# A hybrid decoder step: decode attention in visits of two page tiles, with page loads issued from GpSimd into five buffers

## The chip, the cores and the metric

The kernel runs on one core of a Trainium2 chip. Time is device time of the whole program in microseconds. Engine names: PE is TensorE (matmuls), PEld its weight loads, DVE is VectorE, ACT is ScalarE, POOL is GpSimd, SP is SyncE, whose queue issues most DMAs.

## The reference

One layer of a decoder trunk for a prompt of 512 tokens and 8 samples that each decode one token behind a past of 2048. Cut to the part that the change touches, attention of the samples over their paged caches:

```python
PAST_LEN, PAGE_SIZE, DEC_BATCH, A_HEADS, A_HD = 2048, 128, 8, 4, 64   # 16 pages a sample
...
# k_all, v_all: the cached rows of a sample's pages (by page_table), then the new token's
p1 = jax.nn.softmax(jnp.einsum('bqhd,bkhd->bhqk', qb1, k1f) + bias, axis=-1)
p2 = jax.nn.softmax(jnp.einsum('bqhd,bkhd->bhqk', qb2, k2f) + bias, axis=-1)
return jnp.einsum('bhqk,bkhe->bqhe', p1 - lam * p2, vf)
```

Around it stand a combined projection `z = h @ w_in` (58 column tiles of 128), attention over the prompt, two convolutions, a gated MLP, four gates, a merge, cross attention and a feed-forward network. All inputs are float32.

## The kernel before

Tokens lie along the free dimension, 520 of them (512 and 8), in two halves of 260. A column tile of a weight matrix is 128 columns wide; `gemm` multiplies it in three passes (high by high, high by low, low by high part), 48 matmuls of 260 columns for a full tile, all recorded at L219. Three weight tiles are loaded ahead (`LA`), and ScalarE (L179) and VectorE (L180) split each into its two parts. These tiles form one stream, `order`, and set the pace of TensorE.

Everything else is hung on that stream in stages. `run` emits a column tile, then `take` hands what follows on its sums to a list, and each later tile moves the older ones a stage on. Decode attention is a generator, `decode` (L475 on), and `step(n)` moves it on by n visits. `ZS[n]` says how many visits follow column tile n of the first 26; `G1`, `G3`, `G2` say it for the tiles of three branch gates, where one visit also follows each gate tile.

A visit of the scores part (L500) multiplies one page tile, that is four pages of 128 keys for one sample, by the queries of four heads: four float32 products with 32 rows of output each, into one bank `d`. Each product shows in the trace as two records. After eight samples VectorE takes the bank up (L503). A visit of the values part (L549) multiplies the tile of four pages by the probabilities `Dt`, again four products. There are 32 page tiles of keys and 32 of values, 128 products each. The context `behind()` keeps a product after the newest column tile, but does not keep the four of a visit together; the scheduler of the framework may place products of the prompt's attention (scores L597, transposes L632, values L646, norm L653) or of a norm's column sums (L242) between them. L730 are the transposes of V.

A page tile is loaded by four DMAs of 256 KB (`fetch`, L463 to L466): an entry of the page table `pt` is read into a register, then the DMA is issued, both on the SP queue, in which the loads of the weight tiles (L176) also stand. Page tiles share three buffers (tag `pg`) with the score tile `Sd`, so two hold pages during the scores and three during the values; a load waits for the products that read the buffer before. On GpSimd's queue stand a few fills and four loads of x for a later stage (L1154).

Of the kernel before, what the change touches and what calls it, by code (L numbers as in the profile page):

```python
# [31 lines left out]
ZS = [0, 0, 0, 1, 1, 0, 3, 1, 3, 2, 1, 2, 1, 2, 3, 1, 2, 1, 2, 1, 0, 1, 1, 1, 0, 1]  # L32
WARM = 2
SQ = 4
G2 = [0, 0, 1, 2, 0, 0, 0, 1]
G1 = [1, 0, 1, 0, 0, 0, 1, 0]
G3 = [1, 0, 0, 0, 0, 0, 1, 0]
# [17 lines left out]
# columns of the packed constants  # L55
# [40 lines left out]
def layer(ctx: ExitStack, tc: tile.TileContext, I: dict, O: dict):  # L96
# [12 lines left out]
    # ---------------------------------------------------------------- helpers  # L109
# [73 lines left out]
    def first_weights():  # L183
        """the first tile of the stream, in parts that come between those of x"""
# [18 lines left out]
    def pin():  # L203
        """what VectorE has been given since the last sums were taken up stays behind that."""
# [23 lines left out]
    def gemm(ps, W, xs, first=True, last=True, k0=0, apart=False):  # L228
        """both halves of the tokens; apart: one after the other"""
# [6 lines left out]
    def colsum(mat, srcs):  # L236
        """mat^T (sum of srcs over partitions) in float32: two halves with their columns."""
# [8 lines left out]
    def rsqrt(src, n, v, y, a):  # L246
        """v = (src / n + EPS) ** -0.5, with one Newton step: v (3 - x v^2) / 2."""
# [19 lines left out]
    def rstd(mat, srcs, n, y, v=None):  # L267
        """the reciprocal deviations from column sums; y is scratch."""
# [4 lines left out]
    # ---------------------------------------------------------------- constants  # L273
# [6 lines left out]
    lamt = cst.tile([P, 256], F32, name="lamt")  # L280
# [10 lines left out]
    # ---------------------------------------------------------------- x: split, norm  # L291
# [5 lines left out]
    for i in range(WARM):          # the array's clock rises while the first loads come in  # L297
# [41 lines left out]
    lp = cst.tile([P, 128], F32, name="lamp")  # L339
# [3 lines left out]
    def parameters():  # L343
        """the little columns made from the parameters"""
# [32 lines left out]
    def advance():  # L377
        """the newest sums are taken up, then what is left of the older ones goes a stage on."""
# [10 lines left out]
    def go():  # L389
        """a stage of everything"""  # L390
# [6 lines left out]
    def flush():  # L397
        """everything that is left"""
# [3 lines left out]
    def take(post):  # L402
        """what follows on a tile's sums is begun behind the next tile."""
# [5 lines left out]
    def run(name, i, src, post, steps=0, k0=0, W=None, apart=False):  # L409
        """one column tile"""  # L410
# [7 lines left out]
    def pair(names, src, posts):  # L418
        """the first two column tiles, together while the rows of src come in"""
# [21 lines left out]
    def headnorm(z, sq, mat, n, g):  # L441
        """z * g * rsqrt(mean over the rows of mat's blocks)"""
# [16 lines left out]
    # ---------------------------------------------------------------- paged decode attention  # L459
    last = []  # L460

    def fetch(dst, src, i):
        """dst = the page that entry i of the page table names."""  # L463
        with tc.issue_after(last[-1].ins) if last else nullcontext():
            pid = SP.value_load(pt[0:1, i:i + 1], min_val=0, max_val=159)
        last.append(SP.dma_start(out=dst, in_=src[bass.ds(pid, 1)].rearrange("o p f -> p o f")))  # L466

    def pages():
        return dp.tile([P, 4, 512], F32, tag="pg", name="pg", bufs=3)
# [3 lines left out]
    def decode():  # L473
        Sd = dp.tile([P, 2048], F32, tag="pg", name="Sd", bufs=3)
# [14 lines left out]
        held = [loadk(0)]  # L489
        yield  # L490
        held.append(loadk(1))
        yield
        for n in range(32):
            g, s = n // NS, n % NS
            if s == 0:
                ps = dtile()
            kp = held.pop(0)
            with behind():
                for h in range(4):
                    PE.matmul(ps[32 * h:32 * h + 32, :], lhsT=qz[:, s * 128 + 32 * h:s * 128 + 32 * h + 32],  # L500
                              rhs=kp[:, :, h * P:h * P + P], start=s == 0, stop=s == NS - 1)
            if s == NS - 1:
                V.tensor_tensor_reduce(out=Sd[:, 512 * g:512 * g + 512], in0=ps, in1=cv("dbias"), scale=1.0,  # L503
                                       scalar=-3e38, op0=ALU.add, op1=ALU.max, accum_out=sd[:, g:g + 1])
            held.append(loadk(n + 2) if n < 30 else loadv(n - 30))
            yield
        # the new token's own score
# [32 lines left out]
        held.append(loadv(2))  # L540
        yield
        os_ = []
        for n in range(32):
            if n % 16 == 0:
                ps = dtile()
            vp = held.pop(0)
            with behind():
                for i in range(4):
                    PE.matmul(ps[32 * i:32 * i + 32, :], lhsT=Dt[:, n % 16, :], rhs=vp[:, i, :], start=n % 16 == 0,  # L549
                              stop=n % 16 == 15)  # L550
            if n % 16 == 15:
# [3 lines left out]
            if n + 3 < 32:  # L555
                held.append(loadv(n + 3))
# [44 lines left out]
    def difference(h, qt, ps):  # L601
        """of the two softmaxes"""
# [20 lines left out]
    def turned(h, qt, d):  # L623
        """the keys of one tile of queries on the partitions"""
# [13 lines left out]
    def values(h, pr, dh, dl):  # L638
        """times v, and the norm of the head"""
# [23 lines left out]
    def attention():  # L663
        """a stage a tile: the scores of some queries, the turning of those before, their values, their norm"""
# [71 lines left out]
    # ---------------------------------------------------------------- branch B  # L736
# [43 lines left out]
    def center(ys, ps):  # L780
        """subtracts the mean over the 256 channels of two tiles; returns the squares."""
# [9 lines left out]
    # ---------------------------------------------------------------- branch C  # L791
# [164 lines left out]
    # ---------------------------------------------------------------- gates and merge  # L956
# [35 lines left out]
    def gates(i, br, steps):  # L992
        Wb = None
        for c in range(KT):
            pg_, py = gated(i, c)
            ztile(ZG + 8 * i + c, pg_, 1)
# [470 lines left out]
```

## Time and profile before

| what | value |
|---|---|
| median of three runs | 1075.08 us (1074.6 to 1077.41) |
| span of the profiled execution | 1072.4 us |
| TensorE busy | 1062.6 us (99%) |
| VectorE busy | 594.8 us (55%) |
| ScalarE busy | 457.7 us (43%) |
| GpSimd busy | 4.4 us |

The profiled execution's span counts from its first instruction to its last; the runs' times include what lies around that. A matmul's busy time overlaps that of the next, so the price of a group is read from the start of its first record to the start of what follows.

### The profile page before, as it was taken

How to read it: one execution, taken by the hardware profiler on the slowest of the kernel's cores; microseconds unless marked ns; L12 is line 12 of the kernel's file. 1: busy time of each engine (PE TensorE's matmuls, PEld its weight loads, DVE VectorE, ACT ScalarE, POOL GpSimd, SP SyncE). 2: the span in 40 equal slices, each digit the busy share in tenths (PEclk: the TensorE clock that was granted, in tenths of full speed). 3: DMA queues.
4: the chain of work that ended last, by engine and by line, in shares of the span. 5: the costliest groups of instructions: out<-in, count | busy, mean ns of one | idle time of the engine just before them, and what ended most of it. 6: DMA issues, size and time to landing. Idle time of an engine off the chain costs nothing.

```text
span 1072.4 us, 21375 instructions
## 1 busy us (share of the span) xinstructions
PE 1062.6 (99%) x8434; PEld 962.0 (90%) x8434; DVE 594.8 (55%) x1022; ACT 457.7 (43%) x761; POOL 4.4 (0%) x11
## 2 busy tenths in 40 slices
PE   8999999999999999999999999999999999999998
PEld 7967777878988888888999986999999999999998
DVE  6764665775646665534677678754224424445443
ACT  7754565863412225312555586553223213312320
POOL 0000000000000000000010000000000000000000
PEclk9999999999999999999999999999999999999999
DMA  8667777756567777766432556122232232222231
GB/s 280 239 193 215 218 209 221 237 172 181 178 206 237 236 218 235 218 206 216 148 132 86 202 188 239 41 99 91 87 99 90 90 99 86 93 99 82 96 110 50
DMA packets 73861, 172.06 MB, mean 160 GB/s; under 512 B 9633, under 2 KB 12450, under 8 KB 73634
## 3 DMA queue, kind: packets, MB, share of 16 engines
q1 hardware_dynamic: 73442, 169.65, 50.1%
q8 instruction: 66, 1.08, 0.4%
q0 software_dynamic: 320, 1.07, 0.3%
q14 instruction: 33, 0.27, 0.1%
HBM read 165.07 MB, written 5.61 MB: 159 GB/s over the span
## 4 chain that ended last, share of the span: by engine, by line
PE 96%; ACT 1%; DVE 1%; DMA 0%; SPq 0%; issue 0%; DVEq 0%
PE g L219 80%; PE d L500 4%; PE d L549 3%; PE m L242 2%; PE m L597 1%; PE m L219 1%; PE g L1115 1%; PE m L646 1%; PE m L632 0%; PE m L653 0%; DMA hl<-in_xT 0%; PE m L1261 0%; PE d L1196 0%; ACT t L1266 0%; PE m L730 0%; PE m L534 0%
## 5 line engine op out<-in xcount | busy, mean ns | idle before, releaser
L219 PE MATMUL g<-hl,wh 128*128 128x260 f32 x4332 | 709.2, 285 | 1.2 <-ACT hl L324 0.6
L219 PEld LDWEIGHTS g<-hl,wh 128*128 128x128 f32 x4332 | 595.5, 188 | 51.6 <-issue 18.6
L219 PE MATMUL g<-hl,wl 128*128 128x260 f32 x2166 | 437.0, 283 | 0.0
L219 PEld LDWEIGHTS g<-hl,wl 128*128 128x128 f32 x2166 | 334.1, 188 | 1.9 <-issue 1.7
L179 ACT CAST wh<-w 128x1024 fp32r<-128x1024 f32 x154 | 161.4, 1048 | 395.4 <-PE g L219 309.0
L180 DVE TENSOR_TENSOR wl<-w,wh 128x1024 fp32r<-128x1024 f32 x154 | 188.1, 1222 | 160.9 <-ACT wh L179 151.8
L433 DVE TENSOR_TENSOR t<-g,R 128x520 f32<-128x520 f32 x48 | 33.4, 696 | 76.3 <-PE g L219 76.2
L219 PE MATMUL g<-hb,wh 128*128 128x260 f32 (+1 forms) x436 | 71.1, 282 | 0.0
L219 PEld LDWEIGHTS g<-hb,wh 128*128 128x128 f32 x436 | 60.8, 188 | 0.1
L219 PE MATMUL g<-hb,wl 128*128 128x260 f32 (+1 forms) x218 | 46.6, 283 | 0.0
L500 PE MATMUL d<-pg,qz 128*32 128x512 f32 x256 | 44.9, 604 | 0.4 <-DVE qz L702 0.4
L143 ACT CAST hl<-t 128x520 fp32r<-128x520 f32 (+2 forms) x42 | 24.4, 581 | 43.2 <-DVE t L1331 27.5
L827 DVE SCALAR_TENSOR_TENSOR hl<-uc,cols,hl 128x512 f32<-128x512 f32 x60 | 41.4, 745 | 0.0
L1345 DVE TENSOR_TENSOR hb<-g,hb 128x520 f32<-128x520 f32 x16 | 11.2, 700 | 49.4 <-PE g L219 49.4
L144 DVE TENSOR_TENSOR hl<-t,hl 128x520 fp32r<-128x520 f32 (+2 forms) x42 | 27.0, 644 | 15.8 <-ACT hl L143 15.5
L219 PEld LDWEIGHTS g<-hb,wl 128*128 128x128 f32 x218 | 34.6, 188 | 0.0
L549 PE MATMUL d<-pg,Dt 128*32 128x512 f32 x256 | 33.9, 604 | 0.0
L249 ACT ACTIVATE t<-m,little 128x260 f32<-128x260 f32 (+1 forms) x42 | 19.1, 474 | 26.1 <-PE m L242 13.2
L965 ACT ACTIVATE t<-t 128x520 f32<-128x520 f32 x24 | 15.2, 635 | 27.1 <-DVE t L433 27.0
L254 DVE TENSOR_TENSOR t<-t 128x520 f32<-128x520 f32 (+1 forms) x27 | 15.5, 576 | 19.5 <-ACT t L253 19.1
L1331 DVE TENSOR_TENSOR t<-t 128x520 f32<-128x520 f32 x32 | 22.2, 694 | 0.0
L608 DVE CUSTOM_DVE_ANT_0 t<-m,bias 128x128 f32<-128x128 f32 (+3 forms) x32 | 14.6, 486 | 12.3 <-PE m L597 12.3
(271 smaller groups left out, 818.3 us busy)
## 6 DMA issues: line engine op xcount, KB each, us to landing
pg<-in_kc SPq DMA_DIRECT2D x128, 256.0 KB, 3.4
pg<-in_vc SPq DMA_DIRECT2D x128, 256.0 KB, 3.0
w<-in_win SPq DMA_DIRECT2D x56, 512.0 KB, 4.5
w<-in_wup SPq DMA_DIRECT2D x32, 512.0 KB, 3.3
w<-in_wdn SPq DMA_DIRECT2D x32, 512.0 KB, 3.3
w<-in_wo SPq DMA_DIRECT2D x8, 512.0 KB, 3.3
hl<-in_cmk SPq DMA_DIRECT2D x16, 256.0 KB, 5.2
hl<-in_cmv SPq DMA_DIRECT2D x16, 256.0 KB, 5.5
```

What stands on the lines that cost most here:

```text
L143: S.copy(hi, src)
L144: V.tensor_tensor(out=lo, in0=src, in1=f(hi), op=ALU.subtract)
L179: S.copy(wh, w)
L180: free.add(V.tensor_tensor(out=wl, in0=w, in1=f(wh), op=ALU.subtract).ins.name)
L219: m = PE.matmul(o, lhsT=w, rhs=x[sl], start=first and n == 0, stop=last and n == 2)
L242: PE.matmul(ps[:, 0:H2], lhsT=mat, rhs=s[:, sl], start=i == 0, stop=i == len(srcs) - 1)
L249: S.activation(v[:, sl], i, AF.Identity, scale=-1.0 / n, bias=NEPS)
L433: V.tensor_tensor(out=two(t), in0=gv(ps), in1=two(Rt), op=ALU.mult)
L500: PE.matmul(ps[32 * h:32 * h + 32, :], lhsT=qz[:, s * 128 + 32 * h:s * 128 + 32 * h + 32], rhs=kp[:, :, h * P:h * P + P], start=s == 0, st ...
L549: PE.matmul(ps[32 * i:32 * i + 32, :], lhsT=Dt[:, n % 16, :], rhs=vp[:, i, :], start=n % 16 == 0, stop=n % 16 == 15)
L827: V.scalar_tensor_tensor(out=y[:, 0:NP], in0=u[:, k:k + NP], scalar=cw[:, k:k + 1], in1=y[:, 0:NP], op0=ALU.mult, op1=ALU.add)
L1331: V.tensor_tensor(out=r, in0=r, in1=r, op=ALU.mult)
```

## The change

Visits now take two page tiles: eight products, 16 records, under a raised priority so that the scheduler places nothing between them. There are 16 visits of scores and 16 of values. `fetch` reads the page table and issues the page loads on GpSimd. The tag `pg` has five buffers. `ZS`, `G1`, `G2`, `G3` are new; in the gates visits follow the gate tile alone (`steps[c]`, or every second for the fourth gate). The two parameter tiles `lamt` and `lp` and the tile `Rm` move to shared pools, and the scratch for GpSimd's DMAs is 2048 bytes. Comments are gone, so lines shift by a few: L500 stays, L549 becomes L551, L597 becomes L599, L632 becomes L634, L730 becomes L732.

```diff
-ZS = [0, 0, 0, 1, 1, 0, 3, 1, 3, 2, 1, 2, 1, 2, 3, 1, 2, 1, 2, 1, 0, 1, 1, 1, 0, 1]
+ZS = [0, 0, 0, 1, 0, 1, 1, 1, 1, 1, 1, 1, 1, 1, 1, 1, 0, 1, 1, 1, 0, 1, 1, 0, 1, 0]
...
-            pid = SP.value_load(pt[0:1, i:i + 1], min_val=0, max_val=159)
-        last.append(SP.dma_start(out=dst, in_=src[bass.ds(pid, 1)].rearrange("o p f -> p o f")))
+            pid = GP.value_load(pt[0:1, i:i + 1], min_val=0, max_val=159)
+        last.append(GP.dma_start(out=dst, in_=src[bass.ds(pid, 1)].rearrange("o p f -> p o f")))
...
-        return dp.tile([P, 4, 512], F32, tag="pg", name="pg", bufs=3)
+        return dp.tile([P, 4, 512], F32, tag="pg", name="pg", bufs=5)
...
-            kp = held.pop(0)
-            with behind():
-                for h in range(4):
-                    PE.matmul(ps[32 * h:32 * h + 32, :], lhsT=qz[:, s * 128 + 32 * h:s * 128 + 32 * h + 32],
-                              rhs=kp[:, :, h * P:h * P + P], start=s == 0, stop=s == NS - 1)
+            kps = [held.pop(0) for _ in range(2)]
+            with tc.high_priority(offset=4 * AHEAD), behind():
+                for s, kp in zip((s0, s0 + 1), kps):
+                    for h in range(4):
+                        PE.matmul(ps[32 * h:32 * h + 32, :], lhsT=qz[:, s * 128 + 32 * h:s * 128 + 32 * h + 32],
+                                  rhs=kp[:, :, h * P:h * P + P], start=s == 0, stop=s == NS - 1)
...
-            held.append(loadk(n + 2) if n < 30 else loadv(n - 30))
+            for i in range(2 * v + 4, 2 * v + 6):
+                held.append(loadk(i) if i < 32 else loadv(i - 32))
...
-            ztile(ZG + 8 * i + c, pg_, 1)
+            ztile(ZG + 8 * i + c, pg_, steps[c])
...
-        ztile(ZG + c, post_g0(c), 1)
+        ztile(ZG + c, post_g0(c), c % 2)
...
-    nc = _bacc.Bacc("TRN2", target_bir_lowering=False, num_devices=1)
+    nc = _bacc.Bacc("TRN2", target_bir_lowering=False, num_devices=1, dynamic_dma_scratch_size=2048)
```

The values part changes in the same way as the scores. In the program's order the 128 score products stood in 39 runs (18 of four, 10 of one, 9 of three, one of seven, one of twelve) and now in 16 of eight; the 128 value products in 31 runs (30 of four, one of eight) and now in 16 of eight. The column matmuls stood in 104 uninterrupted runs and now stand in 84. The number of products is 8009 in both.

TensorE, the first visit of decode attention (`qz` are the samples' queries, `pg` a page tile, `d` the bank). Before:

```order
L219 MATMUL g<-hl,wl 128x260 x2
L242 MATMUL m<-t,cc 128x260 x2
L500 MATMUL d<-pg,qz 32x512 x12
L219 MATMUL g<-hl,wh 128x260 x4
L219 MATMUL g<-hl,wl 128x260 x2
```

After:

```order
L219 MATMUL g<-hl,wl 128x260 x2
L500 MATMUL d<-pg,qz 32x512 x8
L242 MATMUL m<-t,cc 128x260 x2
L219 MATMUL g<-hl,wh 128x260 x4
L219 MATMUL g<-hl,wl 128x260 x2
```

The visit moved ahead of the two column sums and has two page tiles in place of three.

TensorE, the score products around the second group of the prompt's scores (`t` holds its probabilities, which L632 turns). Before:

```order
L242 MATMUL m<-t,cc 128x260 x2
L597 MATMUL m<-hl 128x384 x6
L632 MATMUL m<-cc,t 128x128
L500 MATMUL d<-pg,qz 32x512
L632 MATMUL m<-cc,t 128x128 x2
L500 MATMUL d<-pg,qz 32x512 x7
L219 MATMUL g<-hl,wh 128x260 x4
L219 MATMUL g<-hl,wl 128x260 x2
L219 MATMUL g<-hl,wh 128x260 x3
L500 MATMUL d<-pg,qz 32x512 x4
```

After:

```order
L500 MATMUL d<-pg,qz 32x512 x8
L242 MATMUL m<-t,cc 128x260 x2
L599 MATMUL m<-hl 128x384 x6
L634 MATMUL m<-cc,t 128x128
L219 MATMUL g<-hl,wh 128x260 x4
L219 MATMUL g<-hl,wl 128x260 x2
L219 MATMUL g<-hl,wh 128x260 x4
L219 MATMUL g<-hl,wl 128x260
L634 MATMUL m<-cc,t 128x128 x2
```

The single score product between the transposes is gone; matmuls of the column tile stand there.

The queues of the page loads, with the semaphores that each waits for (DMAHW and DMASW count landings of SP's and GpSimd's loads, eight of each in turn; PE and DVE count those engines' work). SP before:

```order
L466 DMA pg<-in_kc 128x512 [waits DMAHW3_49]
L176 DMA w<-in_win 128x1024 [waits DMAHW4_49,DVE_49]
L465 TENSOR_LOAD pt
L465 ISA x2
L466 ISA
L466 DMA pg<-in_kc 128x512 [waits DMAHW5_49]
```

GpSimd after:

```order
L465 DMA pg<-in_kc 128x512 [waits DMASW3_49]
L464 TENSOR_LOAD pt
L464 ISA x2
L465 ISA
L465 DMA pg<-in_kc 128x512 [waits DMASW4_49,PE_49]
```

The table read, its register work and the load moved as they were to GpSimd's queue; weight loads no longer stand between them.

## Rows read from the trace of the kernel before

**Rows 1.** The page: span, busy time by engine, TensorE's granted clock in 40 slices.

```profile
span 1072.4 us, 21375 instructions
...
PE 1062.6 (99%) x8434; PEld 962.0 (90%) x8434; DVE 594.8 (55%) x1022; ACT 457.7 (43%) x761; POOL 4.4 (0%) x11
...
PEclk9999999999999999999999999999999999999999
```

**Rows 2.** The chain that ended last: shares by line; then start us, us, what.

```profile
by line: PE g L219 79.8%; PE d L500 3.9%; PE d L549 3.0%; PE m L242 1.9%; PE m L597 1.2%; PE m L219 1.1%; PE g L1115 0.9%; PE m L646 0.9%; PE m L632 0.5%; PE m L653 0.4%; DMA hl<-in_xT 0.4%; PE m L1261 0.4%; PE d L1196 0.4%; ACT t L1266 0.4
...
33.73 5.74 PE g L219 x48
39.47 1.75 PE m L242 x8
```

**Rows 3.** Timeline, TensorE, one page tile: start us, us, engine line, out<-in, records.

```profile
251.71 0.40 PE L219 MATMUL g<-hl,wl 128*128 128x260 f32 x2
252.04 1.06 PE L500 MATMUL d<-pg,qz 128*32 128x512 f32 x8
253.03 0.75 PE L219 MATMUL g<-hl,wh 128*128 128x260 f32 x4
253.62 0.40 PE L219 MATMUL g<-hl,wl 128*128 128x260 f32 x2
```

**Rows 4.** Timeline, TensorE, value products: two page tiles together.

```profile
487.28 0.40 PE L219 MATMUL g<-hl,wl 128*128 128x260 f32 x2
487.61 1.92 PE L549 MATMUL d<-pg,Dt 128*32 128x512 f32 x16
489.46 0.76 PE L219 MATMUL g<-hl,wh 128*128 128x260 f32 x4
490.06 0.40 PE L219 MATMUL g<-hl,wl 128*128 128x260 f32 x2
```

**Rows 5.** Timeline, TensorE, score products: a page tile split one and three.

```profile
76.05 1.05 PE L500 MATMUL d<-pg,qz 128*32 128x512 f32 x2
77.03 0.44 PE L632 MATMUL m<-cc,t 128*128 128x128 f32 x2
77.39 1.92 PE L500 MATMUL d<-pg,qz 128*32 128x512 f32 x14
79.24 0.74 PE L219 MATMUL g<-hl,wh 128*128 128x260 f32 x4
```

**Rows 6.** Timeline, TensorE, the first run of score products.

```profile
54.40 1.06 PE L500 MATMUL d<-pg,qz 128*32 128x512 f32 x6
55.85 2.76 PE L500 MATMUL d<-pg,qz 128*32 128x512 f32 x18 [0.39 <-DVE qz L702]
58.54 0.74 PE L219 MATMUL g<-hl,wh 128*128 128x260 f32 x4
```

**Rows 7.** Timeline, SyncE's queue: three page loads, nothing else between them.

```profile
240.63 2.56 SPq L466 DMA_DIRECT2D pg<-in_kc  x3
```

**Rows 8.** Line L466, SyncE's page loads: ns min/median/max of the issue.

```profile
L466 SPq DMA_DIRECT2D pg<-in_kc x128: 332/333/955, 23.7 to 264.4; - x128
```

**Rows 9.** Timeline, GpSimd: its four loads in the whole program.

```profile
551.32 2.26 POOL L1154 DMA_DIRECT2D hb<-in_xT  x4
```

**Rows 10.** Line L1154, GpSimd's loads: ns min/median/max, then landing.

```profile
L1154 POOL DMA_DIRECT2D hb<-in_xT x4: 536/536/672, 551.3 to 553.0; - x4
...
DMA to landing us min/median/max: 3.3/3.6/3.9
```

**Rows 11.** Timeline, TensorE: where two groups of V transposes begin.

```profile
64.39 0.27 PE L730 MATMUL m<-cc,t 128*128 128x128 f32 x1
...
140.43 0.27 PE L730 MATMUL m<-cc,t 128*128 128x128 f32 x1
```

**Rows 12.** Groups by line, VectorE, 50 to 145 us: count | busy us, mean ns.

```profile
L433 DVE TENSOR_TENSOR t<-g,R 128x520 f32<-128x520 f32 x8 | 5.5, 692 | 0.0
...
L727 DVE COPY vnew<-t 128x8 f32<-128x8 f32 x3 | 0.5, 162 | 0.0
```

More of the change, by code (lines that the diff above doesn't have):

```diff
@@ L31 @@
 CR = "k0 k1 q0 q1 q2 q3 k2 v0 v1 k3 v2 v3"
-ZS = [0, 0, 0, 1, 1, 0, 3, 1, 3, 2, 1, 2, 1, 2, 3, 1, 2, 1, 2, 1, 0, 1, 1, 1, 0, 1]
+ZS = [0, 0, 0, 1, 0, 1, 1, 1, 1, 1, 1, 1, 1, 1, 1, 1, 0, 1, 1, 1, 0, 1, 1, 0, 1, 0]
 WARM = 2
+G1 = [1, 1, 1, 1, 0, 1, 0, 1]
+G3 = [1, 0, 1, 1, 0, 1, 0, 1]
+G2 = [1, 1, 1, 0, 1, 1, 0, 0]
 SQ = 4
-G2 = [0, 0, 1, 2, 0, 0, 0, 1]
-G1 = [1, 0, 1, 0, 0, 0, 1, 0]
-G3 = [1, 0, 0, 0, 0, 0, 1, 0]
 TB = 10
@@ L279, in layer @@
     stc = cst.tile([P, 2, NS, 30], F32, name="stc")
-    lamt = cst.tile([P, 256], F32, name="lamt")
     pt = cst.tile([1, 128], I32, name="pt")
@@ L338, in layer @@
     lam = cst.tile([P, 8], F32, name="lamc")
-    lp = cst.tile([P, 128], F32, name="lamp")
     LAM, LAMROW = lam[:, 4:5], lam[:, 5:6]
@@ L343, in parameters @@
     def parameters():
+        lamt, lp = T()[:, 0:256], T()[:, 0:128]
         SP.dma_start(out=pt, in_=I["pt"])
@@ L464, in fetch @@
         with tc.issue_after(last[-1].ins) if last else nullcontext():
-            pid = SP.value_load(pt[0:1, i:i + 1], min_val=0, max_val=159)
-        last.append(SP.dma_start(out=dst, in_=src[bass.ds(pid, 1)].rearrange("o p f -> p o f")))
+            pid = GP.value_load(pt[0:1, i:i + 1], min_val=0, max_val=159)
+        last.append(GP.dma_start(out=dst, in_=src[bass.ds(pid, 1)].rearrange("o p f -> p o f")))
     def pages():
-        return dp.tile([P, 4, 512], F32, tag="pg", name="pg", bufs=3)
+        return dp.tile([P, 4, 512], F32, tag="pg", name="pg", bufs=5)
     exps = []
     def decode():
-        Sd = dp.tile([P, 2048], F32, tag="pg", name="Sd", bufs=3)
+        Sd = dp.tile([P, 2048], F32, tag="pg", name="Sd", bufs=5)
         sd = dp.tile([P, 40], F32, tag="sd", name="sd")
@@ L487, in loadv @@
             return vp
-        held = [loadk(0)]
+        held = [loadk(0), loadk(1)]
         yield
-        held.append(loadk(1))
+        held += [loadk(2), loadk(3)]
         yield
-        for n in range(32):
-            g, s = n // NS, n % NS
-            if s == 0:
+        for v in range(16):
+            g, s0 = v // 4, 2 * (v % 4)
+            if s0 == 0:
                 ps = dtile()
-            kp = held.pop(0)
-            with behind():
-                for h in range(4):
-                    PE.matmul(ps[32 * h:32 * h + 32, :], lhsT=qz[:, s * 128 + 32 * h:s * 128 + 32 * h + 32],
-                              rhs=kp[:, :, h * P:h * P + P], start=s == 0, stop=s == NS - 1)
-            if s == NS - 1:
+            kps = [held.pop(0) for _ in range(2)]
[4 more added lines that the diff above has]
+                                  rhs=kp[:, :, h * P:h * P + P], start=s == 0, stop=s == NS - 1)
+            if s0 == NS - 2:
                 V.tensor_tensor_reduce(out=Sd[:, 512 * g:512 * g + 512], in0=ps, in1=cv("dbias"), scale=1.0,
                                        scalar=-3e38, op0=ALU.add, op1=ALU.max, accum_out=sd[:, g:g + 1])
-            held.append(loadk(n + 2) if n < 30 else loadv(n - 30))
+            for i in range(2 * v + 4, 2 * v + 6):
+                held.append(loadk(i) if i < 32 else loadv(i - 32))
             yield
@@ L539, in decode @@
         V.tensor_copy(dn, ps[:, 0:32])
-        held.append(loadv(2))
+        held.append(loadv(4))
         yield
         os_ = []
-        for n in range(32):
-            if n % 16 == 0:
+        for v in range(16):
+            if v % 8 == 0:
                 ps = dtile()
[L546 to L551, printed above, removed]
+            vps = [held.pop(0) for _ in range(2)]
+            with tc.high_priority(offset=4 * AHEAD), behind():
+                for n, vp in zip((2 * v % 16, 2 * v % 16 + 1), vps):
+                    for i in range(4):
+                        PE.matmul(ps[32 * i:32 * i + 32, :], lhsT=Dt[:, n, :], rhs=vp[:, i, :], start=n == 0, stop=n == 15)
+            if v % 8 == 7:
                 ot = T()
@@ L554, in decode @@
                 os_.append(ot)
-            if n + 3 < 32:
-                held.append(loadv(n + 3))
+            for i in range(2 * v + 5, 2 * v + 7):
+                if i < 32:
+                    held.append(loadv(i))
             yield
@@ L1001, in gates @@
                 mpool.append(pool("mp"))
-            Wb = run("wbcd", 2 * (i - 1) + c // 4, br, py, steps[c], k0=2 * (c % 4), W=Wb if c % 4 else None)
+            Wb = run("wbcd", 2 * (i - 1) + c // 4, br, py, 0, k0=2 * (c % 4), W=Wb if c % 4 else None)
     gates(1, bo, G1)
@@ L1043, in layer @@
     ms = []
-    Rm = cst.tile([P, 256], F32, name="Rm")
+    Rm = h2.tile([P, 256], F32, name="Rm")
     Rc = cst.tile([P, 4], F32, name="Rc")
```

## The prediction

> **What bounds the kernel now.** The page comes first [rows 1]: TensorE is busy for 1062.6 of 1072.4 us and its granted clock stands at full speed (2.4 GHz of its two levels) in every slice. The chain of waits agrees [rows 2]: column tiles of the weight stream (L219) hold 79.8% of the span, the score products of decode attention (L500) 3.9%, its value products (L549) 3.0%; DMA has 0.4%, all of it the first load of x. So the program is a queue of TensorE work, and a change is worth what it takes out of that queue, less what it makes TensorE wait for. A column tile of 48 matmuls takes 5.74 us when nothing disturbs it [rows 2], or 0.1196 us each.
>
> **What a visit costs.** Every float32 product of decode attention shows as two records, so a page tile (four products) is 8 records. Look at one alone in a column tile [rows 3]: it starts at 252.04 and the stream goes on at 253.03, 0.99 us later. But the borders cost too. From the last pair ahead (251.71) to the first pair behind (253.62) 1.91 us pass, and the six column matmuls in that stretch need 0.72: the visit's price is 1.19, of which 0.20 are borders. Two page tiles that happen to stand together [rows 4]: 487.61 to 489.46 is 1.85, and 490.06 - 487.28 - 0.72 = 2.06 with borders. So the second page tile costs 0.87, not 1.19. The third price is the surprise of this trace [rows 5]: one single product (2 records) holds TensorE from 76.05 to 77.03, 0.98 us, as long as all four. The seven that follow take 1.85 (77.39 to 79.24), as long as eight, so the three left over cost 0.99. A page tile that is split into one and three pays twice.
>
> **Scores: the sum.** In the order of before the 128 score products stand in 39 runs: 18 of four, 10 of one, 9 of three, one of seven and one of twelve. By the rows this is 18 x 0.99 + 10 x 0.98 + 9 x 0.99 + 1.85 + 4.14 = 42.5 us; the chain's 3.9% of 1072.4 is 41.8, so the count holds. The 4.14 is the first run [rows 6], 54.40 to 58.54: three page tiles in one run are worth 0.99 + 0.86 + 0.86 = 2.71, and 1.43 are a wait, since its fourth product wants the last head's query (qz) and the other three are done too early. In the order of after there are 16 runs of eight: 16 x 1.85 = 29.6. The wait does not go, it grows: the first visit now stands ahead of two L242 products that stood before it. Such a pair takes 0.88 (four of these products, eight records, 1.75 [rows 2]). TensorE gets to the visit that much earlier and qz comes when it came, so I charge 1.43 + 0.88 = 2.3. Scores: 42.5 - 29.6 - 2.3 = 10.6 us saved.
>
> **Values.** 30 runs of four and one of eight before, 30 x 0.99 + 1.85 = 31.6 (the chain: 3.0%, 32.2); 16 x 1.85 = 29.6 after. 2.0 saved.
>
> **Borders.** In the program's order the column stream is cut into 104 runs before and 84 after (same products, 8009 of them in both). Twenty interruptions fewer at 0.20 are 4.0 us. Between zero (if the fewer borders sit beside transposes, where a change of work may cost nothing) and 4.6 (23 score runs fewer) I take 4.0, the price of the plain rows.
>
> **Sum:** 10.6 + 2.0 + 4.0 = 16.6 us.
>
> **What the queues cost.** Taking 256 page loads off SP gives nothing by itself, as no weight load stands in the chain. What matters is whether GpSimd can issue them in time. Each is a table read, some register work and a DMA. On SP three of them cover 2.56 us from the first DMA's start to the last one's end [rows 7], and a DMA takes 0.33 of that [rows 8]: (2.56 - 0.33) / 2 = 1.12 each. All that GpSimd issues in the trace of before is four loads of 260 KB from fixed addresses [rows 9]: 2.26 us for four, 0.536 each at the median, 3.6 us to land [rows 10]. Table reads on GpSimd stand nowhere in this trace, so I bound the price c of one page load there. Below: 0.57, if the reads run ahead while the previous DMA is being written. Above, serial: 1.12 - 0.33 + 0.54 = 1.33. I take the serial end for the test, as the safer.
>
> What c may be follows from the densest stretch. In after the second visit stands right ahead of the first group of V transposes (L730 in before) and the ninth right ahead of the third group; these groups begin at 64.39 and 140.43 in before [rows 11], 76.0 us apart. There before spends 16.7 us on 16 score runs (6 x 0.99, 5 x 0.98, 4 x 0.99, 1.85) and after 7 x 1.85 = 13.0; with about 1 us of borders 71.3 remain for seven visits, 10.2 apart. During the scores four buffers hold pages (the fifth holds the score tile), two visits' worth. The load for visit k may begin when visit k - 2 has read its buffers; GpSimd then needs 8c per visit. From the first visit to the second one L242 pair, one column tile and a visit pass, 0.88 + 5.74 + 2.06 = 8.7 us. Counting from the first visit (k = 0), the pages of the tenth (k = 9) are there after 8 x 8c + 3.6, and it comes after 8.7 + 8 x 10.2 = 90.3. It waits when 64c + 3.6 > 90.3, that is c > 1.35. The tile after it has no visit, and the queue catches up. At 1.33 nothing waits (with 1.6 us to spare), at 1.5 the loss is 9 us, and at c = 1.61 the whole gain of 16.6 is eaten. GpSimd has nothing else to do in this stretch, and behind its last page load stand only a fill and four loads for a later stage. Each load also waits for the eighth one before it to land; 8c is well over 3.6 even at 0.57. The five buffers pay for themselves with room (a smaller DMA scratch, three small tiles moved), which moves no work on TensorE.
>
> **A rule against it.** In the first score stretch VectorE is mostly two-input work of 0.69 us; its plain copies take 0.16 [rows 12]. The Trainium skill, "SBUF — State Buffer", section "Who interferes with whom", says that a GpSimd-issued DMA has its descriptors written through a port that VectorE locks during copies and one-input scalar operations in a fast mode, and that two-input operations leave writes alone. No row here shows it. By that page, as an estimate, a load that met one such copy would wait 0.16 us and be at 1.49, a loss of 9 us inside the first rival below; by the row alone the loss is nothing.
>
> **Rivals.**
> First, supply is tight, or chains come late (chance 0.20). c between 1.35 and 1.6 takes up to 16 us back in the stretch of the first ten visits. Or the transposes of the prompt's attention (L632), which had a split page tile as cover ahead of them, wait for VectorE; the nearest row is the 0.39 us idle at the first visit [rows 6], and at some 16 such places that would be 6 us. For it: VectorE is busy for 55% of the span [rows 1]. Against: ahead of these products the chain gives neither VectorE nor ScalarE a share; the one ScalarE line in it is of cross attention [rows 2]. Either lands between 1062 and 1072; I put it at 1065.
> Second, slower than before (0.10): every GpSimd issue has to wait for one VectorE operation, 0.69 us [rows 12], so c = 1.33 + 0.69 = 2.0. Then the tenth visit is 64 x 2.0 + 3.6 - 90.3 = 41 us late; less 16.6 that is +25, 1100. It decides from c = 1.61 on. Against it speak the four loads of [rows 9, 10], which took 0.54 each.
> Third, the change does not do what it says (0.05): the pair of [rows 4] is a lucky case, and each page tile costs 0.99 wherever it stands. Then 32 x 0.99 = 31.7 replaces each 29.6, the gain falls by 4.2 and the borders' 4.0 go too: 8.4 us are left, 1067. Against: the seven of [rows 5] show the same 0.86 step.
>
> **How the numbers follow.** The profiled span 1072.4 becomes 1055.8. The median of the three runs, 1075.08, lies 2.7 above the span, so 1075.08 - 16.6 = 1058.5. The forecast has 0.63, with its own range of 1055 to 1062 (the borders at 0 on one side, the first wait gone on the other). The full range reaches over most of the first rival and the third: 1054 to 1070; what is left out is the slow case and some 0.08 at the edges. About 0.3% (3.2 us) is what a measurement of this kernel can tell from no change. Faster: 0.63 + 0.05 + most of 0.20, 0.85; same 0.05; slower 0.10.
>
> **What would show it.** In the profile of the changed kernel: L500 and its twin at 2.8% each in the chain; every visit 16 records in 1.85 us; the first one with a wait for qz of about 2.3; no wait of TensorE for a page load; GpSimd's table reads no further apart than 1.35 us when it is not held by a buffer. Wrong would be: TensorE idle ahead of L500 on DMA between 80 and 150 us (supply), or idle at L634 on VectorE or ScalarE (chains).

## The result: 10.9 us saved, 16.6 forecast

The changed kernel takes 1064.3 us (median of four executions, 1061.1 to 1066.7) against 1075.2 for the kernel before: ratio 0.9891, 95% interval 0.9869 to 0.9914. It is 1.1% faster, in the forecast direction and within the range of 1054 to 1070, but 5.8 us above the forecast of 1058.5. Its profiled execution was the longest of the four: span 1065.0, where before's is 1072.4 [rows 1].

**The profile after.** First the page, then the head of the chain that ended last, as in [rows 1, 2]:

```profile
span 1065.0 us, 21390 instructions
...
PE 1049.2 (99%) x8434; PEld 968.2 (91%) x8434; DVE 594.7 (56%) x1022; ACT 455.6 (43%) x759; POOL 142.4 (13%) x267
...
PEclk9999999998899999999999999999999999999999
```

```profile
by line: PE g L219 74.7%; PE d L551 2.8%; PE d L500 2.3%; DMA w<-in_win 1.6%; PE m L242 1.4%; PE m L219 1.1%; PE m L599 1.0%; PE g L1117 0.9%; ACT wh L179 0.7%; issue 0.7%; DVE wl L180 0.6%; ACT t L615 0.5%; ACT t L249 0.4%; PE m L648 0.4%;
```

Two things strike the eye. GpSimd is now busy (its 256 page loads). And TensorE's clock, full in all 40 slices before, is down in the tenth and eleventh, 240 to 293 us; the column stream has lost 5 points of the chain to work that feeds it.

A visit looks as the prediction said. TensorE's timeline, the first visit and the third:

```profile
54.90 3.08 PE L500 MATMUL d<-pg,qz 128*32 128x512 f32 x16
57.91 1.15 PE L242 MATMUL m<-t,cc 128*128 128x260 f32 x4
...
75.00 1.92 PE L500 MATMUL d<-pg,qz 128*32 128x512 f32 x16
76.85 1.14 PE L242 MATMUL m<-t,cc 128*128 128x260 f32 x4
```

76.85 - 75.00 = 1.85, the price of the two page tiles of [rows 4]. All visits but the first score visit and one value visit of 2.01 take it. From each record's start to the next one's, the 256 score records take 30.8 us (42.6 before), the value records 29.8 (31.7 before): 11.75 and 1.9 saved.

So 13.65 us are there in the products alone, and yet the profiled span is only 7.4 shorter. Where the rest went shows when both traces are laid side by side at fixed places of the column stream (start of the product on g that follows the first n, us):

```
n        before    after    after - before
576       114.9    110.3        -4.6
1344      267.0    256.1       -10.9
1536      296.5    294.4        -2.1
3072      522.7    515.3        -7.4   (and the same to the end)
```

Up to the 1344th product all goes as forecast. Between the 1344th and the 1536th, 256 to 294 us in after, 8.8 us are given back. TensorE's timeline there, with its idle time and what ended it:

```profile
256.76 0.64 PE L219 MATMUL g<-hl,wh 128*128 128x260 f32 x4
257.24 0.40 PE L219 MATMUL g<-hl,wl 128*128 128x260 f32 x2
260.17 0.83 PE L219 MATMUL g<-hl,wh 128*128 128x260 f32 x4 [2.53 <-DVE mg L977]
260.79 0.64 PE L219 MATMUL g<-hl,wl 128*128 128x260 f32 x2
261.22 1.07 PE L219 MATMUL g<-hl,wh 128*128 128x260 f32 x4
262.09 0.64 PE L219 MATMUL g<-hl,wl 128*128 128x260 f32 x2
263.52 1.20 PE L219 MATMUL g<-hl,wh 128*128 128x260 f32 x4 [0.80 <-DVE sd L523]
```

TensorE waits for a buffer of sums (g) that VectorE has not taken up: L977 multiplies the branch's sums by the gate. The second wait ends with L523, a step of the softmax's sums; right ahead of it on VectorE stands L432, which takes up a gate's sums (262.69 to 263.38). And after the first wait the same four products take 0.87 us from start to next start (261.22 to 262.09) where they took 0.48 (256.76 to 257.24). ScalarE, at the same time:

```profile
254.42 0.72 ACT L519 ACTIVATE Sd<-Sd,sd 128x512 f32<-128x512 f32 x1 [3.50 <-DVE sd L515]
```

From there the chain that ended last runs through ScalarE and VectorE until TensorE goes on:

```profile
255.24 2.12 ACT Sd L519 x6
...
257.45 1.28 ACT L967
258.75 0.65 ACT t L967
259.41 0.07 DVE mg L977
```

The exponentials of decode attention's softmax (L519, four of 0.7 us) waited until 254.42 for VectorE, where L515 stood among the input work of branch C (L814 to L840); the gate's sigmoid (L967) is ordered behind them in the program, comes with its table load at 257.45 and 258.75, and only then can L977 run. Third, TensorE's busy time and granted clock in stretches of 5 us:

```profile
255.00:260.00 5.00, 2.64 (x23) 1.00 0.24 93
260.00:265.00 5.00, 4.04 (x19) 0.57 0.25 75
265.00:270.00 5.00, 5.00 (x34) 0.75 0.09 33
270.00:275.00 5.00, 5.00 (x44) 0.93 0.12 32
275.00:280.00 5.00, 5.00 (x25) 0.50 0.67 199
```

(Columns: stretch, its length, TensorE busy with records, clock, DMA share, GB/s.) After the idle 2.5 us the clock stands at its lower level (1.2 of 2.4 GHz) from about 261 to 267 us and is full again until 274. Then it is low once more, to 281, and this second time TensorE had been busy since 263.5; what ran there was the row of the sixteen Dt products:

```profile
271.12 3.94 PE L535 MATMUL m<-C,Sd 128*128 128x32 f32 x32
...
275.30 1.21 PE L219 MATMUL g<-hl,wh 128*128 128x260 f32 x4
```

In before every 5 us from 250 to 290 have 5.00 busy and 1.00. Of the 8.8 us, 3.3 are idle time. The visits in this part of the stream weigh about the same in both (after has a pair of value tiles, 1.85; before had one tile of scores and one of values, 1.0 each), so the rest, some 5.5, is the clock. The four executions of after bear this out: mean granted clock 0.994, 0.995, 0.997, 1.000 and spans 1065.0, 1063.4, 1061.8, 1059.4. The one at full clock is 5.6 shorter than the profiled one, and 13.0 below before's profile, 3.6 short of the forecast 16.6: about the idle time.

**Theory:** the visits bring what the sum said; the loss is the softmax, which the new step table puts two gate tiles earlier, among branch C's input work on VectorE and ahead of a gate's sigmoid on ScalarE. **Rivals:** the loss belongs to the visits themselves; or the supply of pages.

### The profile page after: what moved, and what is told of

The parts are those of the page before. It is cut to its first block, busy times and chain, and to the rows that moved or that the text cites. A ratio compares the mean times of both kernels' runs of the same rounds, so it can differ in the third digit from the quotient of the medians.

```text
span 1065.0 us, 21390 instructions
## 1 busy us (share of the span) xinstructions
PE 1049.2 (99%) x8434; PEld 968.2 (91%) x8434; DVE 594.7 (56%) x1022; ACT 455.6 (43%) x759; POOL 142.4 (13%) x267
## 4 chain that ended last, share of the span: by engine, by line
PE 88%; ACT 5%; DVE 3%; DMA 2%; issue 1%; SPq 0%; ACTq 0%; DVEq 0%
PE g L219 75%; PE d L551 3%; PE d L500 2%; DMA w<-in_win 2%; PE m L242 1%; PE m L219 1%; PE m L599 1%; PE g L1117 1%; ACT wh L179 1%; DVE wl L180 1%; ACT t L615 0%; ACT t L249 0%; PE m L648 0%; DMA hl<-in_xT 0%; PE m L1263 0%
## 5 line engine op out<-in xcount | busy, mean ns | idle before, releaser
L219 PE MATMUL g<-hl,wh 128*128 128x260 f32 x4332 | 710.6, 286 | 5.7 <-DVE mg L977 2.5
L219 PEld LDWEIGHTS g<-hl,wh 128*128 128x128 f32 x4332 | 599.7, 189 | 23.6 <-issue 6.4
L219 PE MATMUL g<-hl,wl 128*128 128x260 f32 x2166 | 439.4, 284 | 0.0
L179 ACT CAST wh<-w 128x1024 fp32r<-128x1024 f32 x154 | 161.3, 1048 | 416.1 <-PE g L219 306.8
L219 PEld LDWEIGHTS g<-hl,wl 128*128 128x128 f32 x2166 | 336.2, 190 | 0.2
L180 DVE TENSOR_TENSOR wl<-w,wh 128x1024 fp32r<-128x1024 f32 x154 | 188.1, 1222 | 151.6 <-ACT wh L179 147.8
L465 POOL DMA_DIRECT2D pg<-in_vc x128 | 68.8, 537 | 184.1 <-issue 79.5
L465 POOL DMA_DIRECT2D pg<-in_kc x128 | 69.3, 541 | 146.9 <-issue 101.4
L432 DVE TENSOR_TENSOR t<-g,R 128x520 f32<-128x520 f32 x48 | 33.3, 695 | 68.5 <-PE g L219 68.4
L219 PE MATMUL g<-hb,wh 128*128 128x260 f32 (+1 forms) x436 | 71.1, 282 | 0.0
L219 PEld LDWEIGHTS g<-hb,wh 128*128 128x128 f32 x436 | 60.8, 188 | 0.1
L219 PE MATMUL g<-hb,wl 128*128 128x260 f32 (+1 forms) x218 | 46.6, 283 | 0.0
L219 PEld LDWEIGHTS g<-hb,wl 128*128 128x128 f32 x218 | 34.6, 188 | 0.0
L500 PE MATMUL d<-pg,qz 128*32 128x512 f32 x256 | 31.8, 599 | 0.1
L551 PE MATMUL d<-pg,Dt 128*32 128x512 f32 x256 | 30.8, 598 | 0.0
L249 ACT ACTIVATE t<-m,little 128x260 f32<-128x260 f32 (+1 forms) x42 | 18.9, 474 | 23.8 <-PE m L242 11.5
```

What stands on the lines that cost most here:

```text
L179: S.copy(wh, w)
L180: free.add(V.tensor_tensor(out=wl, in0=w, in1=f(wh), op=ALU.subtract).ins.name)
L249: S.activation(v[:, sl], i, AF.Identity, scale=-1.0 / n, bias=NEPS)
L432: V.tensor_tensor(out=two(t), in0=gv(ps), in1=two(Rt), op=ALU.mult)
L465: last.append(GP.dma_start(out=dst, in_=src[bass.ds(pid, 1)].rearrange("o p f -> p o f")))
L551: PE.matmul(ps[32 * i:32 * i + 32, :], lhsT=Dt[:, n, :], rhs=vp[:, i, :], start=n == 0, stop=n == 15)
```

## The experiments

Times are medians; "before" is the kernel before on the same chip in the same hour, 1075.8 to 1076.7. Ratios are to it.

**1. The softmax two gate tiles later.** In after:

```diff
-G1 = [1, 1, 1, 1, 0, 1, 0, 1]
+G1 = [0, 0, 1, 1, 1, 1, 1, 1]
```

> The kernel after, with the softmax of decode attention (L511 to L520) two gate tiles later, where the kernel before had it; visits, queue and buffers stay. Theory: in the profile of after the softmax's exponentials (L519) wait until 254.4 us for VectorE, hold the gate's sigmoid (L967) and so L977 back, TensorE idles 2.5 and 0.8 us and then runs part of 255 to 282 us at its lower clock; that stretch gave back 8.9 us. Moved, it goes: no wait on L977 of over 0.5 us, granted clock 1.00 from 250 to 300 us, span 1055 to 1058, time 1057 to 1060. Rival: the loss belongs to the visits (the clock falls in this stretch wherever the softmax stands, or the wait only moves with it): span 1062 to 1065, time 1062 to 1066.

1060.7 us, ratio 0.986 (0.984 to 0.988); span 1058.0 in the profile, clock 1.00 from 250 to 300 us. Up to the 1344th product the trace is that of after within 0.6 us; at the 1536th it is 9.0 ahead, at the end 7.0. The span is at the upper end of the theory's range and the time 0.7 above it; its "no wait" failed. TensorE's waits still have

```profile
PE g L219 <- DVE sd L523: 1.7, 1, 1.7
...
PE g L219 <- DVE mg L977: 0.7, 1, 0.7
```

(total us, times, longest). So 2.4 us of idle time are left of 3.3, without a fall of the clock in this execution. Most of the gain over after is the clock: three of the four executions show 1.000, with spans of 1058.0, 1058.5 and 1059.7, and after's one at 1.000 has 1059.4. At equal clock that is about 1 us, the size of the idle time saved. That the later softmax keeps the clock up fits these counts but is not shown by them. The visits are unchanged; whether they bring the rest is left to experiment 5.

**2. Nothing between, but single pages on SyncE's queue.** The kernel before with one thing of the change:

```diff
-            with behind():
+            with tc.high_priority(offset=4 * AHEAD), behind():
                 for h in range(4):
```

(and the same at the value products).

> The kernel before, page loads on SP and visits of one page as they were, with one thing of the change: the products of a page get the priority that keeps other work out. By its order the scores then stand in 29 runs (25 of four, two of eight, one of three and one of nine) instead of 39, and the column stream in 109 runs instead of 104. Theory (a split page tile pays 0.98 us twice): scores 42.5 becomes 25 x 0.99 + 2 x 1.85 + 0.99 + some 3.0 (nine, with its wait) = 32.4, less 10; borders 5 x 0.20 = +1.0; time 1075.2 - 9 = 1066, between 1063 and 1068. Rival (the price is a page tile's, split or not, and only pairs save): time 1074 to 1077.

1068.4 us, ratio 0.993 (0.991 to 0.995). The score records take 32.6 us against 42.6: 10.0 saved, as expected, the time a little above the range, because 3.8 us came in elsewhere, 1.6 of them between the 1344th and the 1536th product, where the clock is down for a moment (0.51 and 0.64 in the stretches from 280 to 284 us). So most of what the change takes out of the score products is the split tile of [rows 5], not the pair. In time the pair is worth about as much: unsplitting gives 8.0 us here (1076.4 to 1068.4), pairs 7.3 in experiments 10 and 11.

**3. After, with its page loads on SyncE's queue.**

```diff
-            pid = GP.value_load(pt[0:1, i:i + 1], min_val=0, max_val=159)
-        last.append(GP.dma_start(out=dst, ...
+            pid = SP.value_load(pt[0:1, i:i + 1], min_val=0, max_val=159)
+        last.append(SP.dma_start(out=dst, ...
```

> The kernel after with its page loads issued from SP again, as in before (five buffers and pair visits stay; by its order two of the 16 score visits fall into two runs of four). Theory of the prediction: the queue gives nothing by itself while loads come in time; time within 3 us of after (1061 to 1067), 0.3 us lost by the two split visits. Rival (SP's weight loads queue behind page loads that wait for a buffer, which is what the queue was changed for): TensorE waits for L219's weights by DMA, 5 us or more, time 1069 or more.

1075.5 us, ratio 0.999 (0.998 to 1.001): the whole gain is gone, as the rival had it. SyncE's queue in the dense stretch (start, us, line):

```profile
146.32 8.72 SPq L465 DMA_DIRECT2D pg<-in_kc  x8
155.15 0.38 SPq L176 DMA_DIRECT2D w<-in_win  x1
156.35 8.13 SPq L465 DMA_DIRECT2D pg<-in_kc  x8
```

Between two weight loads eight page loads now stand, 8 us of issue and more where they wait for a buffer. Whether weights are early can be read from SyncE's own waits between 60 and 240 us. In after it waits 98.6 us for the buffer that L180 frees (weights as far ahead as the buffers allow), in before 12.5, here 6.8:

```profile
SPq L465 <- PE d L500: 8.5, 4, 5.5
...
SPq L176 <- DVE wl L180: 6.8, 1, 6.8
```

TensorE's waits then show what after does not have:

```profile
PE g L219 <- ACT wh L179: 2.9, 1, 2.9
...
PE g L219 <- DVE wl L180: 1.6, 4, 0.5
```

From the 576th to the 960th column product this kernel falls 10.9 us behind after, and the clock is down to 0.78 between 170 and 180 us. The rival's path is right in part: these waits are 4.5 us, not 5 or more, and none ends with a load. The longest ends with a cast (L179) at 175.42, whose weights had been issued at 164.59 and had landed at 170.6; it stood behind a norm's chain on ScalarE (L249 to L252, from 173.23). That the planner put it there because weights come later is likely, not shown.

**4. GpSimd's loads made dearer.** In after, each load reads its table entry three times:

```diff
+            GP.value_load(pt[0:1, i:i + 1], min_val=0, max_val=159)
+            GP.value_load(pt[0:1, i:i + 1], min_val=0, max_val=159)
             pid = GP.value_load(pt[0:1, i:i + 1], min_val=0, max_val=159)
```

> The kernel after, but each page load on GpSimd reads its table entry three times instead of once. A load's price on the queue in after is 1.18 us (0.54 + 0.64 by the timeline); two more reads of 0.28 to 0.35 make it 1.75 to 1.9. By the prediction's formula, with the tenth visit 91.5 us behind the first as measured in after, TensorE waits at visits of L500 by 64 x 1.75 + 3.6 - 91.5 = 24 to 64 x 1.9 + 3.6 - 91.5 = 34 us in all: time 1088 to 1098. Rival (the supply has more room than the formula says, since loads run ahead of the visit that frees their buffer): under 10 us lost, time below 1074.

1223 us. The direction is the theory's, the size is far off, for two reasons. A read costs 0.57 us, not 0.3: the median distance of two loads is 1.19 us in after and 2.33 here, (2.33 - 1.19) / 2. And the order was planned anew: the products of score and value now stand in 75 runs, not 32. So the formula for the tenth visit was not tested with the visits it was made for. What it does show is the queue as the bound: the last load is issued at 639 us, at 470 in after, and the 169 between them are about the 159 us lost. TensorE's waits name it, with half of that time (the more numerous runs and a mean clock of 0.961 stand beside it):

```profile
PE d L502 <- DMA pg<-in_kc: 60.8, 19, 8.7
PE d L553 <- DMA pg<-in_vc: 15.4, 13, 2.3
```

**5. All softmax steps where before had them.** Experiment 1 left the softmax's sums one whole gate tile behind its exponentials; before had half a tile:

```diff
-G1 = [1, 1, 1, 1, 0, 1, 0, 1]
+G1 = [0, 0, 1, 1, 1, 1, 0, 1]
...
-            Wb = run("wbcd", ..., br, py, 0, ...)
+            Wb = run("wbcd", ..., br, py, int(i == 1 and c == 2), ...)
```

> The kernel after with all three softmax steps where before had them: exponentials at the third gate tile of the first branch, its sums (L522 to L528) half a tile behind them at the branch's own product, Dt one tile on. In the run with only the first of these moved TensorE still waited 1.7 us for DVE sd L523 and 0.7 us for DVE mg L977. Theory (the place of the softmax against the gate's sigmoid is all of it): the 1.7 goes, the 0.7 may stay, granted clock 1.00; span 1055.5 to 1057, time 1057.5 to 1060. Rival (the wait moves to whatever stands next on VectorE): span 1058 or more, time 1060 to 1062.

1059.3 us (1056.3 to 1060.6), ratio 0.984 (0.982 to 0.985). Both waits, on L523 and on L977, are gone, with the visits as in after: the rival that the visits bring the loss falls. The median lies in the theory's range, the profiled span (1058.9) above it. In this execution the clock fell with TensorE busy throughout, while the sixteen Dt products (L535, 32 columns each) ran from 272.3 us on:

```profile
272.00:274.00 2.00, 2.00 (x21) 1.00 0.04 8
274.00:276.00 2.00, 2.00 (x17) 0.80 0.00 0
276.00:278.00 2.00, 2.00 (x10) 0.50 0.35 84
```

So this fall is not the softmax's waits. An execution of the same kernel whose mean clock was 1.000 has a span of 1054.7; after's at 1.000 has 1059.4. The place of the softmax is thus worth 4.7 us without the clock (one execution of each).

**6. Single pages on GpSimd's queue.** Experiment 2 with the queue of after (the edit of experiment 3 the other way), three buffers.

> Visits of one page that nothing splits, three buffers, as in the second experiment (1068.35), with the page loads issued from GpSimd. By its order the scores stand in 26 runs (21 of four, four of eight, one of twelve): 21 x 0.99 + 4 x 1.85 + 4.0 = 32.2 against 32.6 measured there; five interruptions of the column stream fewer at 0.20 = 1.0. Theory of the prediction (the queue gives nothing by itself): 1066 to 1069. Rival (page loads on SP hold weight loads back, with single pages too): 2 us or more below that, 1062 to 1065.

1071.1 us, 2.7 more than experiment 2; neither expectation. The queue not only gives nothing, it costs: with three buffers two page tiles are in hand, and TensorE waits for pages,

```profile
PE d L500 <- DMA pg<-in_kc: 1.8, 4, 0.9
```

**7. The queue alone.** The kernel before with that one edit, no priority.

> The kernel before with one edit: page loads issued from GpSimd, visits of one page, no priority, three buffers. By its order the scores stand in 34 runs instead of 39 (17 of four, eight of one, three of seven, three of three, one each of eight, twelve and two): 17 x 0.99 + 8 x 0.98 + 3 x 1.85 + 3 x 0.99 + 1.85 + 4.1 + 0.98 = 40.1 against 42.5; four interruptions of the stream fewer, 0.8. Theory of the prediction (the queue gives nothing by itself): 3 us below before, 1072 to 1074. Rival (the queue is worth what page loads on SP cost the weights): 1063 to 1069.

1078.5 us, ratio 1.003 (1.002 to 1.005): 2.7 slower than before, though its scores are cut less often. TensorE waits here too,

```profile
PE d L500 <- DMA pg<-in_kc: 2.0, 3, 0.8
```

so single pages get a little less than nothing from the queue. Both expectations missed: the theory had 1072 to 1074. The score records do take 2.9 us less than in before (39.7 against 42.6), as it had summed; the value records take 0.8 more and the stream's 2.8 more, and why the stream does is open.

**8. Four buffers instead of five.**

```diff
-        return dp.tile([P, 4, 512], F32, tag="pg", name="pg", bufs=5)
+        return dp.tile([P, 4, 512], F32, tag="pg", name="pg", bufs=4)
```

(and for the score tile, which has the same tag). TensorE's order is that of after, instruction by instruction.

> The kernel after with four page buffers instead of five (three hold pages during the scores); TensorE's order is the same. A load may then begin when the page three before it has been read. With 1.19 to 1.26 us a load, 3 to 4.3 us to land and the visits' places in the trace of after, my sum leaves at most 1 us of waiting at two visits. Theory (supply has that much room): 1062 to 1067, as after. Rival (the fifth buffer is what keeps TensorE from waiting): waits of over 1 us for a page at most visits of the dense stretch, 1072 or more.

1065.6 us, ratio 0.990 (0.988 to 0.992), as after. One wait for a page is left,

```profile
PE d L500 <- DMA pg<-in_kc: 0.9, 1, 0.9
```

of the size the sum gave. The fifth buffer is worth about that; the ranges of the two kernels overlap (1064.2 to 1068.5 here), so the times tell no more.

**9. Dt in two groups.** Experiment 5 with the sixteen Dt products as eight and eight, half a tile apart (and a step more in the gate loop for the second group):

```diff
-            for q in range(16):
+            for q in range(8):
                 PE.matmul(ps[:, 32 * q:32 * q + 32], lhsT=Sd[...], rhs=C, ...)
+        yield
+        with behind():
+            for q in range(8, 16):
+                PE.matmul(ps[:, 32 * q:32 * q + 32], lhsT=Sd[...], rhs=C, ...)
```

> The kernel of the fifth experiment with the sixteen Dt products (L535, 32 columns each, 3.6 us in a row) in two groups of eight, half a tile (12 column products) apart. In the profiles of after and of the second, fifth and sixth experiments the granted clock fell to its lower level for 3 to 6 us right behind that row, in those of before and of the first experiment it did not. Theory (the row of narrow products brings the clock down): with half of it at a time granted clock 1.00 from 260 to 300 us and at least 0.999 in all runs, 2 us less than the fifth experiment, 1056 to 1058, one interruption more being 0.2. Rival (it falls in some executions whatever stands there): clocks between 0.996 and 1.000 again, 1057 to 1060.

1057.0 us (1056.6 to 1057.7), ratio 0.982 (0.981 to 0.983), the best of all. It is to be read with 11.

**10. Pairs undone.** After with visits of one page, its queue, its five buffers, its priority; steps as before.

> The kernel after with its pairs undone: GpSimd queue, five buffers, priority as in after, visits of one page, steps and softmax where before had them. By its order the scores stand in 23 runs (16 of four, five of eight, two of twelve): 16 x 0.99 + 5 x 1.85 + 2 x 2.7 + 1.2 of waiting = 31.7, against 30.8 measured in after; the values 31.7 against 29.8; the column stream in 105 runs instead of 84, 21 x 0.20 = 4.2. Theory (a page tile alone costs its 0.99 and its two borders): 7.0 us more than the kernel of the fifth experiment (1059.3), 1064 to 1068. Rival (borders cost nothing, pairs save only the products' 2.8): 1061 to 1063.

1066.4 us, ratio 0.991 (0.989 to 0.993), 7.3 above experiment 11 on the same chip; the theory said 7.0. In the traces the products are 3.4 dearer (1.5 and 1.9), and the column stream's records 3.5 for 21 interruptions more. Waits and falls of the clock in either trace are in the 3.5; behind the 1536th product, where only one short fall in 10 disturbs it, it is 2.6 for 15 interruptions, 0.17 each.

**11. Experiment 5 again,** unchanged, beside 9 and 10.

> The kernel of the fifth experiment again, on the same chip as the ninth and tenth, to compare with them: 1057.5 to 1060.5, with some runs at a granted clock of 1.000 (span 1054 to 1056) and some at 0.996 to 0.998 (span 1057 to 1059).

1059.1 us (1058.2 to 1060.0), clocks 0.997 to 0.998. Experiment 9 is 2.0 lower, and their executions don't overlap. But its theory is not shown: in this profile the undivided row of Dt was followed by products at full speed,

```profile
273.89 3.65 PE L535 MATMUL m<-C,Sd 128*128 128x32 f32 x32
277.38 0.39 PE L539 MATMUL m<-C,t 128*128 128x32 f32 x2
277.60 0.73 PE L219 MATMUL g<-hl,wh 128*128 128x260 f32 x4
```

(277.60 to 278.40, where the next group of four begins, is the full-speed step after a change of work), and the two profiled executions differ elsewhere: 2.4 us between the 192nd and the 384th column product, 33 to 71 us, where this one waits 1.8 us for L249 and then has a fall of the clock (0.97 over its first 50 us). The difference goes with the clock: 9 shows 0.998 to 1.000, and its executions at 1.000 (1055.0, 1055.3, 1055.8) are no shorter than the one of experiment 5 at 1.000 (1054.7). Why 9 kept the clock more often stays open.

## Why the prediction was right and where it failed

**The scores (10.6 forecast, 11.75 measured).** The counts and prices of [rows 3 to 6] hold: 16 runs of 1.85 and a wait. Experiment 2 shows that unsplitting alone is 10.0 of it. Off was the first visit's wait for qz, 2.3 forecast and 1.16 measured (3.01 - 1.85). The step that failed is "TensorE gets to the visit that much earlier": it got there at 54.90, 0.50 later than before (54.40), although a pair of sums fewer stood ahead, because it had waited already: up to the visit it was idle for 4.5 us, in before for 2.9. The longest piece of it after the first 20 us:

```profile
40.66 0.71 PE L219 MATMUL g<-hl,wh 128*128 128x260 f32 x3
42.26 0.70 PE L242 MATMUL m<-t,cc 128*128 128x260 f32 x2 [0.89 <-ACT t L249]
```

**The values (2.0 forecast, 1.9 measured)** and the **borders' price (0.20)** are right. From the 1536th product on, where 15 value runs stand in place of 30, the stream's records take 2.6 us less, 0.17 for each of 15 interruptions; experiment 10 gave 0.17. But the whole 4.0 is not to be seen in the sum: in the scores' stretch the saving up to the 1344th product, 10.9, is what the products alone save there (10.8): waits like the one above took the borders' share. One of them is the prediction's "chains late" at the place it named, though 0.5 us in all and not 6:

```profile
PE m L634 <- DVE s L610: 0.5, 2, 0.3
```

**The step that failed: the softmax was left out.** The sum has terms for scores, values and borders, and none for the third part of decode attention between them. The change's step tables (ZS, G1) were read for where the visits stand; the same tables also move L511 to L528 two gate tiles forward, onto branch C's input work on VectorE and ahead of a sigmoid whose result frees TensorE's sums. The prediction looked for late chains at L634 and for idle time ahead of L500; it came at L219, from L977 and L523. Experiments 1 and 5 put the softmax back, with the value visits behind it a little moved and no other edit: 3.6 and 5.0 us less than after in the medians, both waits gone in 5, which is 4.7 less at a clock of 1.000. The sum also had no term for the clock: it read full speed off before's profile and kept it, where after's executions lose up to 5.6 us by it. The first fall follows the wait that the softmax made; the second, behind the Dt products, came in experiment 5 without any wait, so only part of this can be put down to the softmax. With the softmax where it was, the sum comes out: forecast span 1055.8; experiment 5 had 1054.7 in the execution with a clock of 1.000, and experiment 9 spans of 1055.0 to 1056.0. Medians of 1059.3 and 1057.0 stand beside the forecast's 1058.5.

**The queue.** The price c of a page load was bounded at 0.57 to 1.33 and the serial end taken. It is serial and a little cheaper:

```profile
60.06 0.54 POOL L465 DMA_DIRECT2D pg<-in_kc  x1 [0.65 <-issue]
61.24 0.54 POOL L465 DMA_DIRECT2D pg<-in_kc  x1 [0.65 <-issue]
```

1.18 from one to the next, a table read of 0.29 and register work inside the 0.65. The tenth visit comes 91.5 us after the first (90.3 forecast), its pages need 64 x 1.19 + 3.6 = 80 (81 with the 4.7 us that a score page took to land at the median). No page load stands in the list of TensorE's waits in after, as said. That the queue "gives nothing by itself" is right for before's visits (experiments 6, 7) and misses the point of the change: pairs on SyncE's queue bring nothing at all (experiment 3). The prediction asked whether GpSimd could bear the loads, and not whether SyncE could have borne them in eights.

**The rule against it.** The Trainium skill, "SBUF — State Buffer", section "Who interferes with whom", would let a load meet VectorE's copies. The issue of a page load on GpSimd took 536 ns at the least and at the median in all 256, as in [rows 10], 753 at the most, with VectorE busy for 56% of the span: by these rows hardly an issue was held up, and the 9 us estimated from the page did not appear.

**The other rivals.** The slow case (c = 2) fell with c = 1.19; experiment 4 shows that it was real: at 2.33 the queue is the bound. "The pair is a lucky case" fell: all 32 visits are pairs and 30 of them take 1.85. The time came out where the first rival had been put (1065), but for another reason: the range held by luck as far as the loss goes, since neither the softmax nor the clock stood in it.

## What to carry to other kernels

When a change rewrites a table of steps, list everything that moves with it, not the steps that it is about: here a short chain on VectorE and ScalarE between two stages cost 4.7 us at full clock, a third of the 13.65 that the stages gained, and falls of the clock behind it and behind the next stage took up to 5.6 more. A gain from fewer, longer visits has a condition in the queue that feeds them: loads that come in eights must not stand ahead of the weights in the same queue, while for single pages the other queue was 2.7 us slower. Price a split before a pair: keeping the four products of a page tile together gave 10.0 of the 11.75 us in the score products; what pairs add lies in the borders and the values as well.

## What was not expected of the hardware

- The clock cost more than the wait. In after a wait of 2.5 us was followed by some 6 us at the lower level, and the row of Dt products, with no wait, by some 7 more; together some 5.5 us were lost. Experiment 1 had waits of 0.7 and 1.7 us at the same place and kept 1.00; 11 had one of 1.8 us near 43 us and a fall behind it. In experiment 5 the clock fell with TensorE busy all the time; in the same kernel's other profile (11) it did not at that place. What decides is not settled here.
- Executions of one kernel differed by up to 6.6 us in span (experiment 7: 1074.5 to 1081.1). In after the spans, 1059.4 to 1065.0, stand in the order of their mean clock.
- A second table read on GpSimd costs 0.57 us, twice what its own record (0.28 at the median) shows.
